# Output projection as seven half-size products over pairs of token blocks, in a hybrid decoder layer

## The chip, the cores and the metric

The kernel runs on one core of a Trainium2 chip (trn2). The metric is the device time of one execution in microseconds (us). Engines: TensorE (PE, its weight loads PEld), VectorE (DVE), ScalarE (ACT), GpSimd (POOL) and SyncE (SP), which here only issues DMAs. Each engine works through its own queue in order.

## What is computed

One layer of a decoder with two token mixers side by side, T = D = 1024, all in float32:

```
h = rmsnorm(x, norm_g);  proj = h @ w_in          # q, k, v, gates, decay code, merge gates
y_a = (gla(...) * silu gate) @ w_pa               # gated linear attention, 4 heads
y_b = (stick_breaking(...) * silu gate) @ w_pb    # 8 heads
merged = g_a * y_a + g_b * y_b
out = rmsnorm(x + merged @ w_o, final_g)
```

The change concerns `merged @ w_o` and what follows, and where its operands are made.

## The kernel before

Every float32 operand of a large product is split into a high part (ScalarE copies it as fp32r, `split` line 153) and a low part (VectorE subtracts, line 154); a product is then three matmuls, high x high, high x low and low x high. Activations are kept as four quarters of 512 x 512: two halves of the tokens by even and odd blocks of 128 rows of D (`quarter`, `quads_in`).

The stages in order of time: norm and value projections (to about 210 us); the **pair stage**, in which 24 `pair_job`s compute 256 columns of `proj` each (to about 730 us); the stick-breaking stage (`scores`, `turn`, `values`), with the w_pa product beside it; the **w_pb stage** (`m_half`, line 989, 16 units of 24 matmuls), and the **w_o stage** (from line 1002).

A `pair_job` (line 218) already computes its product by seven half-size products instead of eight, with sums of weights and sums of activations (T1 to T4, S1 to S4): `load` loads 1 MB of w_in into `raw` and makes four sums on GpSimd into `tt` (lines 228 to 231; there is one `tt` buffer, so the sums wait until VectorE has split those of the job before), and `unit(0..6)` are seven products of twelve matmuls. `Pairs.run` (line 65) hands out units, splits and loads. `pairs.run(24)` (line 619) runs the first 24 units; then the gated linear attention (GLA) begins between further units: `gl_half` (line 647) loads `qe` and `ke` and lets GpSimd multiply `qe` into `q2` (line 658), `gl_local` (line 673) begins with the products `pa` (lines 678, 679), of which every first one needs `q2` and `ke`.

Where no `manual_schedule` stands, a scheduler places the instructions of an engine, by its own estimate of when they are ready; with it an engine keeps the order of the program. A pool that is closed gives its memory to the next one; a new tile waits only for the users of the tiles that lay in the same place (`reuse_waits="tile"`).

In the w_o stage of before, the 128 tokens of a block are the stationary operand and w_o moves past: first 256 columns for all eight blocks (`proj_n`, lines 205 to 207), then 512 and 256 columns for each. `finish` (line 1019) adds x, squares for the norm, multiplies by final_g; then come the power on GpSimd (line 1043), the scaling and the stores.

Of the kernel before, what the change touches and what calls it, by code (L numbers as in the profile page):

```python
# [15 lines left out]
P = 128  # L16
# [78 lines left out]
def hybrid_layer(ctx: ExitStack, tc: tile.TileContext, x, norm_g, w_in, w_up, b_dec,  # L95
# [20 lines left out]
    def dram_set(nm, count, shape, dt=F32):  # L116
        return [dram.tile(shape, dt, tag=f"{nm}{i}", name=f"d_{nm}{i}") for i in range(count)]
# [10 lines left out]
    d_a21 = dram_set("a21", 2, [P, 4, HALF])  # L128

# [489 lines left out]
    pairs.run(24)  # L619
# [337 lines left out]
    pq = ctx.enter_context(tc.tile_pool(name="pq", bufs=1, reuse_waits="tile"))  # L957
    pb_ctx = ExitStack()
# [5 lines left out]
    mq = {}  # L964
# [22 lines left out]
    mq.update(quads_in(a21b, "m"))  # L987

    def m_half(pt, eb, n):
        o = stage().bitcast(F32)  # L990
# [20 lines left out]
    wB = [[po.tile([P, D - DV], F32R, tag=f"wo{s}{k}", name=f"wo{s}{k}", bufs=1) for k in range(KB)]
          for s in "hl"]
    ygA = po.tile([P, NT, DV], F32, tag="ygA", name="ygA", bufs=1)
    for kb in range(KB):
        raw = raw_tile().rearrange("p a b -> p (a b)")[:, 0:D - DV]
        nc.sync.dma_start(raw, w_o[kb * P:(kb + 1) * P, DV:D])
        split(raw, wB[0][kb], wB[1][kb])

    def finish(tb, k, c0, pt, y, yg):

        n = y.shape[-1]
        nc.vector.tensor_add(y, pt, y)
        junk = ps.tile([P, HALF], F32, tag="tr", name="junk")
        nc.scalar.activation(junk[:, 0:n], y, AF.Square, accum_out=ssq[:, tb, k:k + 1])
        nc.vector.tensor_mul(yg, y, fg[:, c0:c0 + n])

    for tb in range(NT):
        finish(tb, 0, 0, proj_n(wsA, mq, tb), xA[:, tb], ygA[:, tb])
    for tb in range(NT):
        ts = slice(tb * P, (tb + 1) * P)  # L1030
        y = po.tile([P, D - DV], F32, tag="y", name="y")
        nc.sync.dma_start(y, x2[ts, DV:D])
        yg = po.tile([P, D], F32, tag="yg", name="yg")
        nc.gpsimd.tensor_copy(yg[:, 0:DV], ygA[:, tb])
        for k, (c0, n) in ((1, (DV, HALF)), (2, (DV + HALF, DV))):
            a = c0 - DV
            pt = proj_n(lambda kb: (wB[0][kb][:, a:a + n], wB[1][kb][:, a:a + n]), mq, tb, n)
            finish(tb, k, c0, pt, y[:, a:a + n], yg[:, c0:c0 + n])
# [33 lines left out]
```

## Time and profile before

| | us |
|---|---|
| median of 3 timed runs (1262.37 to 1264.12) | 1262.98 |
| the profiled execution, its own time | 1259.98 |
| its span, first to last instruction | 1258.3 |
| TensorE busy | 1234.0 |
| VectorE busy | 753.4 |
| ScalarE busy | 519.8 |
| GpSimd busy | 243.3 |

Times of rows are microseconds from the start of the span. Matmuls overlap in a row's duration (0.39 us for 512 columns), so their pace is read from one start to the next. "[13.91 <-DVE wl L154]" behind a row is the idle time of its engine in front of it and what ended it. A granted clock of 1.00 is TensorE's full 2.4 GHz, 0.50 is its lower level, 1.2 GHz.

### The profile page before, as it was taken

How to read it: one execution, taken by the hardware profiler on the slowest of the kernel's cores; microseconds unless marked ns; L12 is line 12 of the kernel's file. 1: busy time of each engine (PE TensorE's matmuls, PEld its weight loads, DVE VectorE, ACT ScalarE, POOL GpSimd, SP SyncE). 2: the span in 40 equal slices, each digit the busy share in tenths (PEclk: the TensorE clock that was granted, in tenths of full speed). 3: DMA queues.
4: the chain of work that ended last, by engine and by line, in shares of the span. 5: the costliest groups of instructions: out<-in, count | busy, mean ns of one | idle time of the engine just before them, and what ended most of it. 6: DMA issues, size and time to landing. Idle time of an engine off the chain costs nothing.

```text
span 1258.3 us, 18805 instructions
## 1 busy us (share of the span) xinstructions
PE 1234.0 (98%) x6947; PEld 1054.5 (84%) x6947; DVE 753.4 (60%) x1309; ACT 519.8 (41%) x1024; POOL 243.3 (19%) x280
## 2 busy tenths in 40 slices
PE   8999999999999999999999999999999999999998
PEld 8999999888888888888888877777777878888986
DVE  5682454545667666666564357778887775444533
ACT  5454332344344444444444444545644443122322
POOL 2400471323223233232323010000100000000010
PEclk9999999999999999999999999999999999999999
DMA  7547353534644565655433765444775437543232
GB/s 270 186 142 269 126 181 133 188 116 149 192 157 137 188 208 173 215 179 177 159 117 121 246 206 160 135 163 147 220 245 175 135 109 265 190 161 110 85 116 92
DMA packets 176982, 212.09 MB, mean 169 GB/s; under 512 B 11222, under 2 KB 129004, under 8 KB 174332
## 3 DMA queue, kind: packets, MB, share of 16 engines
q1 hardware_dynamic: 175740, 209.34, 50.8%
q10 hardware_dynamic: 1152, 1.57, 0.3%
q8 instruction: 54, 0.88, 0.3%
q14 instruction: 36, 0.29, 0.1%
HBM read 133.28 MB, written 77.59 MB: 168 GB/s over the span
## 4 chain that ended last, share of the span: by engine, by line
PE 84%; DVE 8%; DMA 3%; ACT 2%; issue 2%; SPq 0%; POOL 0%; DVEq 0%; POOLq 0%; ACTq 0%
PE pp L254 12%; PE pp L256 12%; PE pp L255 12%; PE pp L207 7%; PE pp L205 7%; PE pp L206 7%; PE pp L193 6%; PE pp L194 6%; PE pp L192 5%; DVE eb L828 3%; PE av L864 1%; DVE be L833 1%; PE tr L847 1%; PE av L865 1%; PE av L863 1%
## 5 line engine op out<-in xcount | busy, mean ns | idle before, releaser
L153 ACT ACTIVATE wh<-raw 128x1024 fp32r<-128x1024 f32 x57 | 60.4, 1060 | 125.8 <-PE pp L193 69.6
L154 DVE TENSOR_TENSOR wl<-tt,wh 128x1024 fp32r<-128x1024 f32 x48 | 58.8, 1224 | 69.3 <-ACT wh L153 69.1
L291 DVE TENSOR_TENSOR f<-pp,f 128x512 f32<-128x512 f32 x72 | 49.7, 690 | 81.2 <-PE pp L256 77.9
L154 DVE TENSOR_TENSOR wl<-raw,wh 128x1024 fp32r<-128x1024 f32 x57 | 78.2, 1371 | 29.4 <-ACT wh L153 28.4
L153 ACT ACTIVATE wh<-tt 128x1024 fp32r<-128x1024 f32 x48 | 50.9, 1061 | 75.7 <-PE pp L255 69.0
L830 POOL TENSOR_SCALAR_AFFINE_SELECT be<-be 128x128 f32<-128x128 f32 x64 | 23.0, 360 | 277.1 <-ACT be L822 211.1
L828 DVE TENSOR_TENSOR_SCAN eb<-eb 128x128 f32<-128x128 f32 (+6 forms) x56 | 71.8, 1282 | 5.6 <-ACT eb L821 3.1
L154 DVE TENSOR_TENSOR o<-pp,o 128x256 fp32r<-128x256 f32 (+1 forms) x72 | 32.4, 451 | 66.1 <-ACT o L153 63.0
L153 ACT ACTIVATE o<-pp 128x256 fp32r<-128x256 f32 (+1 forms) x72 | 29.0, 403 | 93.5 <-PE pp L207 90.3
L821 ACT ACTIVATE eb<-z 128x384 f32<-128x384 f32 (+4 forms) x96 | 48.4, 506 | 44.6 <-PE z L819 30.7
L260 ACT ACTIVATE f<-pp 128x512 f32<-128x512 f32 x72 | 42.5, 590 | 55.8 <-PE pp L256 55.8
L228 POOL TENSOR_TENSOR tt<-raw 128x512 f32<-128x512 f32 x24 | 31.2, 1302 | 150.4 <-DVE wl L154 135.8
L153 ACT ACTIVATE ath<-tr 128x512 fp32r<-128x512 f32 (+2 forms) x96 | 44.0, 496 | 38.8 <-PE tr L847 37.9
L215 POOL TENSOR_TENSOR r<-r,nhalf 128x1 f32<-128x1 f32 x40 | 23.4, 586 | 188.3 <-DVE r L214 188.3
L154 DVE TENSOR_TENSOR atl<-tr,ath 128x512 fp32r<-128x512 f32 (+2 forms) x96 | 51.1, 546 | 5.3 <-ACT ath L153 5.3
L864 PE MATMUL av<-atl,v 128*128 128x256 f32 x160 | 47.0, 293 | 3.9 <-DVE atl L154 3.9
L847 PE MATMUL tr<-ident,be 128*128 128x128 f32 x288 | 44.5, 278 | 5.8 <-DVE be L833 4.9
L847 PEld LDWEIGHTS tr<-ident,be 128*128 128x128 f32 x288 | 32.5, 140 | 20.7 <-DVE be L833 11.2
L192 PE MATMUL pp<-bh,wh 128*128 128x512 f32 x128 | 49.9, 390 | 0.0
L193 PE MATMUL pp<-bl,wh 128*128 128x512 f32 x128 | 49.9, 390 | 0.0
L194 PE MATMUL pp<-bh,wl 128*128 128x512 f32 x128 | 49.9, 390 | 0.0
L833 DVE TENSOR_TENSOR be<-be,eb 128x128 f32<-128x128 f32 (+3 forms) x64 | 48.3, 755 | 1.9
(406 smaller groups left out, 4177.2 us busy)
## 6 DMA issues: line engine op xcount, KB each, us to landing
raw<-in_w_in_dram SPq DMA_DIRECT2D x31, 1024.0 KB, 5.9
d_v<-o SPq DMA_DIRECT2D x32, 256.0 KB, 3.2
d_gv<-o SPq DMA_DIRECT2D x16, 512.0 KB, 2.7
v<-d_gv SPq DMA_DIRECT2D x32, 256.0 KB, 3.1
d_q<-o SPq DMA_DIRECT2D x16, 512.0 KB, 5.7
d_k<-o SPq DMA_DIRECT2D x16, 512.0 KB, 3.9
k<-d_k SPq DMA_DIRECT2D x8, 1024.0 KB, 5.0
v<-d_v SPq DMA_DIRECT2D x8, 1024.0 KB, 6.6
```

The costliest lines, as they stand in the source:

```text
L153: nc.scalar.activation(hi, src, AF.Copy)
L154: eng.tensor_sub(lo, src, hi.bitcast(F32))
L192: nc.tensor.matmul(pt, whi[:, kb], h_, start=kb == 0, stop=False)
L193: nc.tensor.matmul(pt, whi[:, kb], l_, start=False, stop=False)
L194: nc.tensor.matmul(pt, wlo[:, kb], h_, start=False, stop=kb == KB - 1)
L205: nc.tensor.matmul(pt[:, 0:n], h_, whi, start=kb == 0, stop=False)
L206: nc.tensor.matmul(pt[:, 0:n], h_, wlo, start=False, stop=False)
L254: nc.tensor.matmul(pt, bh[:, j], ah[:, j], start=first and j == 0, stop=False, skip_group_check=True)
L255: nc.tensor.matmul(pt, bh[:, j], al[:, j], start=False, stop=False, skip_group_check=True)
L256: nc.tensor.matmul(pt, bl[:, j], ah[:, j], start=False, stop=j == 3, skip_group_check=True)
L828: nc.vector.tensor_tensor_scan(rest, rest, rest, om[:, T - P:T - P + 1], op0=ALU.mult, op1=ALU.min)
L847: nc.tensor.transpose(pt[:, b * P:(b + 1) * P], be[:, c:c + P], ident)
```

## The change

The product `merged @ w_o` is now made as in a pair job, for all tokens: with the four quarters of `merged` (A11, A12, A22 and the sums S1 to S4) as stationary and those of w_o (B11, B21, B22 and the sums T1 to T4) as moving operands, seven products of 512 x 512 x 512, each in four items of twelve 512-column matmuls (one item for each block of 128 tokens of a half). The fourth product (S1 T1) and the fifth (S4 B22) alternate.

The sums T1 to T4 of w_o are made in the first 24 units of the pair stage: w_o comes in four pieces of 1 MB (pairs of row blocks) into the new pool `tq`, GpSimd makes four subtractions in each and the results go to DRAM. GpSimd keeps program order there. Sums S1 to S4 of `merged` are made on GpSimd in the w_pb stage, whose last units change places, and go through DRAM too. In the last stage loads, splits and evictions are placed by hand between the items.

```diff
-    pairs.run(24)
...
+    tq_ctx = ExitStack()
+    tq = tq_ctx.enter_context(tc.tile_pool(name="tq", bufs=2, reuse_waits="tile"))
...
+    def t_sums(j, part):
+        a = wt[j]
+        for dst, x1, x2_ in (((0, 1, 0), (1, 3, 1)), ((3, 3, 0), (2, 2, 3)))[part]:
+            nc.gpsimd.tensor_sub(a[:, dst], a[:, x1], a[:, x2_])
+
+    def t_store(j):
+        for i, nm in enumerate(("T1", "T3", "T4", "T2")):
+            nc.sync.dma_start(d_t[nm][j // 2][:, j % 2], wt[j][:, i])
...
+        for at, fn in ((0, lambda j: t_load(j)), (5, lambda j: t_sums(j, 0)), (6, lambda j: t_sums(j, 1)),
+                       (8, lambda j: t_store(j))):
+            tjobs[5 * j + at].append((fn, j))
+    with tc.manual_schedule(engines={mybir.EngineType.Pool}):
+        for jobs in tjobs:
+            pairs.run(1)
+            for fn, j in jobs:
+                fn(j)
+    tq_ctx.close()
...
+        m = ms[j, n, e] = mo.tile([P, HALF], F32, tag="m", name="m")
         nc.vector.tensor_mul(o[:, 0], pt, o[:, 0])
-        nc.vector.tensor_add(o[:, 0], o[:, 0], o[:, 1])
-        q = mq[n, eb % 2]
-        split(o[:, 0], q[0][:, eb // 2], q[1][:, eb // 2])
+        nc.vector.tensor_add(m, o[:, 0], o[:, 1])
+        if n == 0:
+            hi, lo = op[("A11", "A12")[e]]
+            split(m, hi[:, j], lo[:, j])
...
+    def m_sums(j):
+        return [m_sum(j, "S1", (1, 0), (1, 1), ALU.add), m_sum(j, "S2", "S1", (0, 0), ALU.subtract),
+                m_sum(j, "S4", (0, 1), "S2", ALU.subtract), m_sum(j, "S3", (0, 0), (1, 0), ALU.subtract)]
...
+    def y_load(n, t):
+        ys[n, t] = (po.tile([P, D], F32, tag="ya", name="ya", bufs=4) if n == 0 or t == 3 else
+                    py.tile([P, D], F32, tag="y", name="y"))
+        r0 = n * HALF + t * P
+        nc.sync.dma_start(ys[n, t], x2[r0:r0 + P, :])
...
+    def product(bank, a, b, t, first):
+        (ah, al), w = op[a], op[b]
+        cs = slice(t * P, (t + 1) * P)
+        for j in range(4):
+            bh, bl = (v[:, j % 2] for v in w[j // 2]) if isinstance(w, list) else (v[:, j] for v in w)
+            nc.tensor.matmul(bank, ah[:, j, cs], bh, start=first and j == 0, stop=False, skip_group_check=True)
+            nc.tensor.matmul(bank, ah[:, j, cs], bl, start=False, stop=False, skip_group_check=True)
+            nc.tensor.matmul(bank, al[:, j, cs], bh, start=False, stop=j == 3, skip_group_check=True)
...
+    items = ([(u, t) for u in range(3) for t in range(4)] + [(3, 0), (3, 1), (4, 0), (3, 2), (4, 1), (3, 3), (4, 2), (4, 3)] +
+             [(u, t) for u in (5, 6) for t in range(4)])
...
+    for k, it in enumerate(items):
+        item(*it)
+        mine = [items[e] for e in ev_at.get(k, [k])]
+        for e in mine:
+            evict_a(*e)
+        for e in late:
+            evict_c(*e)
+        for nm, js in parts.get(k, []):
+            o_lo(nm, js)
+        if k in loads:
+            o_load(*loads[k])[0]()
+        his(k + 1)
+        for e in mine:
+            evict_b(*e)
+        late = mine
+        if k == 15:
+            y_load(1, 3)
```

`evict_a` adds an item's bank to the rows of x (VectorE) and squares finished halves (ScalarE), `evict_b` makes the factor of the norm, `evict_c` scales by it and by final_g and stores. `parts` and `loads` say after which item an operand is split and loaded.

How the instructions move. GpSimd at the second pair job of before (`tt` are a job's four sums, `q` is q2, `tri` and `am` are masks of the GLA):

```order
L625 MEMSET tri 128x128
L630 MEMSET am_3022 64x64
L630 MEMSET am_3023 64x64
L626 AFFINE_SELECT tri<-tri 128x128
L228 TENSOR_TENSOR tt<-raw 128x512
L230 TENSOR_TENSOR tt<-raw 128x512
L229 TENSOR_TENSOR tt<-raw,tt 128x512
L231 TENSOR_TENSOR tt<-raw,tt 128x512
L658 TENSOR_TENSOR q_3033<-qe,fac 128x512
```

and the same engine now, from the fifth pair job's sums on (`t` are the sums of w_o):

```order
L231 TENSOR_TENSOR tt<-raw 128x512
L232 TENSOR_TENSOR tt<-raw,tt 128x512
L233 TENSOR_TENSOR tt<-raw 128x512
L234 TENSOR_TENSOR tt<-raw,tt 128x512
L637 TENSOR_TENSOR t<-t 128x512 x8
L659 MEMSET tri 128x128
L664 MEMSET am_3091 64x64
L664 MEMSET am_3092 64x64
L660 AFFINE_SELECT tri<-tri 128x128
L692 TENSOR_TENSOR q_3102<-qe,fac 128x512
L231 TENSOR_TENSOR tt<-raw 128x512
```

The masks and q2 stood right behind the sums of the second pair job; they now stand behind those of the fifth and eight subtractions for w_o.

SyncE at the loads of `qe` and `ke` before (`f`, `d_e`: decay factors; `d_gq`, `d_gk`: q and k of the GLA in DRAM):

```order
L583 DMA f_2724<-d_e20_128 128x512
L656 DMA qe_3260<-d_gq0_116 128x512
L585 DMA d_gk0_120<-f_2724 128x512
L657 DMA ke_3034<-d_gk0_120 128x512
L583 DMA f_2778<-d_e21_129 128x512
```

(`qe` there is the second half's; the first one's load is twelve rows up) and now, with what each waits for:

```order
L607 DMA d_ga0_144<-o_3057 128x512 [waits DMAHW0_49,Activation_49]
L641 DMA d_tT11_171<-t_2914 128x512 [waits DMAHW1_49,Pool_49]
L641 DMA d_tT31_175<-t_2914 128x512 [waits DMAHW2_49,Pool_49]
L641 DMA d_tT41_177<-t_2914 128x512 [waits DMAHW3_49,Pool_49]
L641 DMA d_tT21_173<-t_2914 128x512 [waits DMAHW4_49]
L690 DMA qe_3101<-d_gq0_116 128x512 [waits DMAHW7_49,DMAHW6_49,DMAHW5_49]
L691 DMA ke_3103<-d_gk0_120 128x512 [waits DMAHW3_49,DMAHW4_49,DMAHW2_49,DMAHW1_49]
L700 DMA v_3107<-d_gv0_132 128x512
```

Both loads went behind the stores of the w_o sums (`d_tT`), and `ke` waits for four of them (the semaphores DMAHW1 to DMAHW4).

TensorE at the GLA's first product before (`S3`, `S4`, `ha22`: the fifth to seventh unit of the fourth pair job):

```order
L254 MATMUL pp_2959<-S3h_1595,wh_2955 128x512
L255 MATMUL pp_2959<-S3l_1596,wh_2955 128x512
L256 MATMUL pp_2959<-S3h_1595,wl_2956 128x512
L678 MATMUL pa_3081<-q2_3033,ke_3034 64x128
L679 MATMUL pa_3081<-qe_3032,ke_3034 64x64
L691 MATMUL tr_3092<-ident_170,k2_3090 128x128
L254 MATMUL pp_3042<-S4h_1703,dh_2935 128x512
L255 MATMUL pp_3042<-S4l_1704,dh_2935 128x512
```

and now:

```order
L258 MATMUL pp_3111<-S4l_1722,dh_2994 128x512
L259 MATMUL pp_3111<-S4h_1721,dl_2995 128x512
L257 MATMUL pp_3020<-ha22h_220,wh_3016 128x512
L258 MATMUL pp_3020<-ha22l_221,wh_3016 128x512
L712 MATMUL pa_3150<-q2_3102,ke_3103 64x128
L713 MATMUL pa_3150<-qe_3101,ke_3103 64x64
L259 MATMUL pp_3020<-ha22h_220,wl_3017 128x512
L257 MATMUL pp_3020<-ha22h_220,wh_3016 128x512
L725 MATMUL tr_3161<-ident_188,k2_3159 128x128
```

`pa` stood between the fifth and the sixth unit; it now stands behind the second matmul of the seventh.

SyncE at the end of the kernel before (`y`: rows of x):

```order
L1046 DMA out_dram<-yg 128x640
L1032 DMA y<-in_x_dram 128x768
L1046 DMA out_dram<-yg 128x640
L1032 DMA y<-in_x_dram 128x768
L1046 DMA out_dram<-yg 128x640
L1032 DMA y<-in_x_dram 128x768
L1046 DMA out_dram<-yg 128x640 x3
```

and now (`ya`, `y`: rows of x, in which the output is made):

```order
L1079 DMA raw<-d_sA_186 128x1024
L1079 DMA raw<-d_sA_187 128x1024
L1183 DMA out_dram<-ya 128x1024
L1137 DMA ya<-in_x_dram 128x1024
L1183 DMA out_dram<-ya 128x1024 x3
L1183 DMA out_dram<-y 128x512 x3
L1183 DMA out_dram<-ya 128x512
```

One load of x stands between the first and the second store of the output; the others come before all stores.

## Rows read from the trace of the kernel before

**Rows 1.** The page: busy time, share of the span and instructions of each engine; and the chain of work that ended last, by engine.

```profile
PE 1234.0 (98%) x6947; PEld 1054.5 (84%) x6947; DVE 753.4 (60%) x1309; ACT 519.8 (41%) x1024; POOL 243.3 (19%) x280
...
PE 84%; DVE 8%; DMA 3%; ACT 2%; issue 2%; SPq 0%; POOL 0%; DVEq 0%; POOLq 0%; ACTq 0%
```

**Rows 2.** The table of busy times by stretch: most of the w_pb stage, and the later part of the w_o stage. Columns: stretch, its length, then for each engine the busy time and (x) its instructions; granted clock, DMA share, GB/s.

```profile
1062.00:1158.00 96.00, 96.00 (x425) 79.51 (x424) 42.28 (x56) 18.80 (x24) 0.00 (x0) 1.00 0.50 165
1180.00:1252.00 72.00, 72.00 (x423) 63.42 (x421) 27.14 (x58) 15.12 (x43) 6.23 (x13) 1.00 0.24 84
```

**Rows 3.** The timeline of TensorE: the last 30 matmuls of the w_pb stage from their first, the first of the w_o stage, the first of a group of 24 matmuls of 512 columns in it and the first of the 256-column group behind, and the last matmul of the kernel. Columns: start, duration, engine, line, operation, out<-in, shape.

```profile
1154.62 0.39 PE L192 MATMUL pp<-bh,wh 128*128 128x512 f32 x1
...
1161.19 0.39 PE L194 MATMUL pp<-bh,wl 128*128 128x512 f32 x1
1161.42 0.28 PE L205 MATMUL pp<-wh,ma11h 128*128 128x256 f32 x1
...
1235.10 0.39 PE L205 MATMUL pp<-woh,ma21h 128*128 128x512 f32 x1
...
1240.67 0.28 PE L205 MATMUL pp<-woh,ma21h 128*128 128x256 f32 x1
...
1251.85 0.28 PE L207 MATMUL pp<-woh,ma22l 128*128 128x256 f32 x1
```

**Rows 4.** The timeline of the other engines at the end: a 512-column piece (add, square, the next small operation), and the last piece up to its scaling.

```profile
1249.31 0.69 DVE L1022 TENSOR_TENSOR y<-pp,y 128x512 f32<-128x512 f32 x1 [3.10 <-PE pp L207]
...
1250.04 0.60 ACT L1024 ACTIVATE junk<-y 128x512 f32<-128x512 f32 x1 [3.77 <-DVE y L1022]
...
1250.80 0.21 DVE L1040 TENSOR_SCALAR pre<-ssq 128x1 f32<-128x1 f32 x1
...
1252.16 0.42 DVE L1022 TENSOR_TENSOR y<-pp,y 128x256 f32<-128x256 f32 x1 [1.15 <-PE pp L207]
...
1253.16 0.21 DVE L1042 TENSOR_SCALAR r<-ssq,pre 128x1 f32<-128x1 f32 x1
1253.52 0.55 POOL L1043 TENSOR_TENSOR r<-r,nhalf 128x1 f32<-128x1 f32 x1 [7.90 <-DVE r L1042]
...
1254.10 0.61 ACT L1047 ACTIVATE yg<-yg,r 128x384 f32<-128x384 f32 x1 [0.97 <-POOL r L1043]
```

**Rows 5.** The timeline of TensorE: the first matmul of the pair stage, the first product of the GLA, and the first matmul of the seventh unit of the fourth pair job.

```profile
209.65 0.40 PE L254 MATMUL pp<-ha11h,wh 128*128 128x512 f32 x1
...
280.49 0.32 PE L678 MATMUL pa<-q,ke 128*64 128x128 f32 x1
...
283.75 0.39 PE L254 MATMUL pp<-ha22h,wh 128*128 128x512 f32 x1
```

**Rows 6.** The timeline of GpSimd: one sum of the first pair job, and the first and the last of the four sums of the fifth.

```profile
165.31 1.75 POOL L230 TENSOR_TENSOR tt<-raw 128x512 f32<-128x512 f32 x1
...
269.25 1.30 POOL L228 TENSOR_TENSOR tt<-raw 128x512 f32<-128x512 f32 x1 [13.91 <-DVE wl L154]
...
273.12 1.29 POOL L231 TENSOR_TENSOR tt<-raw,tt 128x512 f32<-128x512 f32 x1
```

**Rows 7.** The timelines of SyncE, GpSimd and VectorE around the GLA's first loads: a store to DRAM and the load that waits for it, for qe and for ke, and the first user of each.

```profile
216.83 0.32 SPq L585 DMA_DIRECT2D d_gq<-f  x1
218.84 0.32 SPq L656 DMA_DIRECT2D qe<-d_gq  x1
...
222.02 1.79 POOL L658 TENSOR_TENSOR q<-qe,fac 128x512 f32<-128x512 f32 x1 [5.96 <-DMA qe<-d_gq]
...
236.87 0.32 SPq L585 DMA_DIRECT2D d_gk<-f  x1
238.87 0.32 SPq L657 DMA_DIRECT2D ke<-d_gk  x1
...
241.88 0.28 DVE L688 TENSOR_TENSOR k<-ke,fac 128x128 f32<-128x128 f32 x1
```

**Rows 8.** The DMA issues by line (count, KB each, median us from issue to landing), and for ke's loads the shortest, median and longest.

```profile
xt<-in_x_dram SPq DMA_DIRECT2D x8, 512.0 KB, 7.5
...
y<-in_x_dram SPq DMA_DIRECT2D x8, 384.0 KB, 3.0
out_dram<-yg SPq DMA_DIRECT2D x8, 320.0 KB, 3.0
...
DMA to landing us min/median/max: 2.6/3.6/7.5
```

**Rows 9.** The table by stretch (columns as in rows 2; the granted clock is the third number from the end) after the last matmul, and the timeline of TensorE's first matmuls in the kernel, which only keep it busy (`warm`).

```profile
1254.00:1255.00 1.00, 0.00 (x0) 0.00 (x0) 0.55 (x1) 0.61 (x1) 0.07 (x1) 1.00 0.00 0
1255.00:1256.00 1.00, 0.00 (x0) 0.00 (x0) 0.00 (x0) 0.00 (x0) 0.00 (x0) 0.62 0.49 189
1256.00:1257.00 1.00, 0.00 (x0) 0.00 (x0) 0.00 (x0) 0.00 (x0) 0.00 (x0) 0.50 0.91 335
...
1.43 5.31 PE L137 MATMUL warm<-ident 128*128 128x128 f32 x26 [1.43 <-POOL ident masks.py:199]
...
8.95 2.40 PE L137 MATMUL warm<-ident 128*128 128x128 f32 x20
```

**Rows 10.** VectorE: two splits of 1024 columns in the timeline, the first beside GpSimd's sums of rows 6; and the scaling of 1024 columns by a factor and a row, in the table of groups by line (busy time, mean ns of one).

```profile
273.30 2.20 DVE L154 TENSOR_TENSOR wl<-raw,wh 128x1024 fp32r<-128x1024 f32 x1
278.80 1.23 DVE L154 TENSOR_TENSOR wl<-tt,wh 128x1024 fp32r<-128x1024 f32 x1 [3.30 <-ACT wh L153]
...
L374 DVE SCALAR_TENSOR_TENSOR xs<-xt,r,gb 128x1024 f32<-128x1024 f32 x8 | 10.2, 1278 | 1.4 <-POOL r L215 1.4
```

More of the change, by code (lines that the diff above doesn't have):

```diff
@@ L962, in b_dma @@
         reload_dma((d_osb[2 * j], d_osb[2 * j + 1]), j)
-    mq = {}
     def pb_load(eb):
@@ L1013, in hybrid_layer @@
[L1013 to L1025, printed above, removed]
@@ new lines, in m_stores, with go, o_load @@
+    def m_stores(j, nms=("S2", "S1", "S4", "S3", "A22")):
+        def go():
+            for nm in nms:
+                nc.sync.dma_start(d_s[nm][j // 2][:, j % 2], ms[j, nm] if nm[0] == "S" else ms[j, 1, 1])
+        return (go, False)
+    WQ = {"B11": (0, 0), "B21": (1, 0), "B22": (1, 1)}
+    def o_load(nm, tag="raw", js=(0, 4)):
+        def go():
+            raw = (raw_tile().rearrange("p k c -> p (k c)") if tag == "raw" else
+                   sw.tile([P, 4, 4, P], F32, tag="tt", name="tt", bufs=1).rearrange("p q a c -> p (q a c)"))
+            oraw[nm] = raw = raw.rearrange("p (j c) -> p j c", j=4)
+            for i in range(2):
+                n = min(js[1] - 2 * i, 2)
+                if nm in WQ:
+                    e, J = WQ[nm]
+                    src = (w_o.rearrange("(j two p) c -> two p j c", two=2, p=P)
+                           [e][:, 2 * i:2 * i + 2, J * HALF:(J + 1) * HALF])
+                else:
+                    src = (d_t if nm[0] == "T" else d_s)[nm][i][:]
+                nc.sync.dma_start(raw[:, 2 * i:2 * i + n], src[:, 0:n])
+        return (go, False)
@@ new lines, in hybrid_layer @@
+    for k, (eb, n) in enumerate(order):
+        if n == 0 and eb + 2 < KB:
+            line.append(pb_load(eb + 2))
+        line.append(pb_unit(eb, n))
+        if k % 4 == 3:
+            line += m_sums(k // 4)
+        if k % 4 == 0 and k:
+            line.append(m_stores(k // 4 - 1))
+        line += extra.get(k, [])
+    Line(line).run()
+    pb_ctx.close()
+    mo_ctx.close()
+    po = ctx.enter_context(tc.tile_pool(name="po", bufs=1, side="right", reuse_waits="tile"))
+    py = ctx.enter_context(tc.tile_pool(name="py", bufs=3, reuse_waits="tile"))
@@ new lines, in fresh_bank, with add, square, factor @@
+    def fresh_bank():
+        return ps.tile([P, HALF], F32, tag="pp", name="pp", bufs=3)
+    def add(n, t, J, bank):
+        y = ys[n, t][:, half(J)]
+        nc.vector.tensor_add(y, bank, y)
+    def square(n, t, J):
+        i = n * 4 + t
+        junk = ps.tile([P, HALF], F32, tag="av", name="junk", bufs=1)
+        nc.scalar.activation(junk, ys[n, t][:, half(J)], AF.Square, accum_out=ssq[:, i, J:J + 1])
+    def factor(n, t, J):
+        i = n * 4 + t
+        if (n, t) not in pre:
+            pre[n, t] = pq.tile([P, 2], F32, tag="pre", name="pre", bufs=8)
+            nc.vector.tensor_scalar(pre[n, t][:, 0:1], ssq[:, i, J:J + 1], D * EPS, None, op0=ALU.add)
+        else:
+            r = pre[n, t][:, 1:2]
+            nc.vector.tensor_scalar(r, ssq[:, i, J:J + 1], pre[n, t][:, 0:1], 1.0 / D, op0=ALU.add, op1=ALU.mult)
+            nc.gpsimd.tensor_tensor(r, r, nhalf, op=ALU.pow)
@@ new lines, in put, with scale, evict_a @@
+    def put(n, t, eng, cols):
+        r0 = n * HALF + t * P
+        eng.dma_start(o2[r0:r0 + P, cols], ys[n, t][:, cols])
+    def scale(n, t, cols):
+        y = ys[n, t][:, cols]
+        nc.vector.scalar_tensor_tensor(y, y, pre[n, t][:, 1:2], fg[:, cols], op0=ALU.mult, op1=ALU.mult)
+    WHERE = [(0, 0), (0, 0), (0, 1), (1, 1), (0, 1), (1, 1), (1, 0)]
+    def evict_a(u, t):
+        n, J = WHERE[u]
+        add(n, t, J, zb.pop(t) if u in (1, 4) else zb[t] if u == 3 else xb[t])
+        if u in (1, 4, 5, 6):
+            square(n, t, J)
@@ new lines, in item, with t3 @@
+    def item(u, t):
+        if u in (1, 3):
+            zb[t] = fresh_bank()
+        bank = zb[t] if u in (1, 3, 4) else xb[t]
+        product(bank, *(("A11", "B11"), ("A12", "B21"), ("S2", "T2"), ("S1", "T1"), ("S4", "B22"), ("S3", "T3"),
+                        ("A22", "T4"))[u], t, u in (0, 1, 3))
+    def t3():
+        return [tuple(sw.tile([P, KB, P], F32R, tag=tag, name=tag).rearrange("p k c -> p (k c)")
+                      .rearrange("p (j c) -> p j c", j=2) for tag in ("wh", "wl")) for _ in range(2)]
@@ L1051 @@
+    manual.close()
 _INS = ["x", "norm_g", "w_in", "w_dec_up", "b_dec", "gla_norm_g", "w_pa", "w_pb", "b_gate",
```

131 lines of the change are left out of this document (97 added, 34 removed).

## Prediction

> **What bounds the kernel now.** First the page's busy times and its chain of waits: TensorE is busy 98% of the span and the chain that ended last runs over it for 84% [rows 1]. Then the table by stretch: in the w_pb stage and in the w_o stage TensorE is busy all the time at full granted clock, while VectorE fills less than half of either [rows 2]. So what counts is how many matmuls there are, how far apart they start, and each stall of TensorE's queue, which works in program order. Nothing behind a stalled matmul can overtake it.
>
> **What the change removes.** In the timeline of TensorE the w_o stage begins at 1161.42 and its last matmul starts at 1251.85, which with its own 0.12 is 90.55 us [rows 3]. It has 8 token blocks x 8 row blocks x 3 = 192 matmuls of 512 columns and 384 of 256. The new stage has 7 products x 4 token blocks x 4 x 3 = 336 matmuls of 512 columns and nothing else. What one costs: in the stage just before, which is a pure stream of 512-column matmuls, 30 of them take 1161.42 - 1154.62 = 6.80 us, 0.2267 each; in the mixed stream of the old w_o stage 24 took 1240.67 - 1235.10 = 5.57, 0.2321 each [rows 3]. The new stream is pure, so I take 0.2267: 76.2 us. The other end is 78.0. Term: **-14.4**, up to -12.6.
>
> **The tail.** Before, the add started 0.31 after the start of the last matmul; the final scaling starts at 1254.10, 2.13 after the end of the matmuls at 1251.97, and takes 0.61: 2.74 [rows 4]. Now the last piece has 512 columns: 0.2, add 0.69, square until the next small VectorE operation 0.76 (1250.04 to 1250.80), from there to the power on GpSimd 0.36 and to the scaling 0.58, scaling 0.69 [rows 4]: 3.3. Term: **+0.6**. Output DMAs are of the same size as before.
>
> **Sums of w_o in the pair stage.** Sixteen GpSimd subtractions, 4 MB loaded and 4 MB stored. GpSimd waited 13.91 us in front of one of the pair jobs' sums [rows 6], so their time would be free. Their place is not. As the order shows, GpSimd now does the eight subtractions of the third and fourth pair of w_o rows right behind the sums of the fifth pair job, and the first multiplication of the gated linear attention (GLA) behind them; SyncE issues the GLA's loads of qe and ke behind the stores of these sums, ke even waits until the last store has landed, since it takes the same memory. Before, qe was loaded at 218.84 and ke at 238.87 [rows 7].
> By rows: the fifth job's sums start at 269.25, set off by VectorE freeing their buffer, which the change does not move, and end at 273.12 + 1.29 = 274.41, 5.16 for four [rows 6]. Eight more end at 284.7. Two stores are then issued, the second at 285.2. A store of that size lets a load that waits for it go 2.0 us later (216.83 to 218.84, 236.87 to 238.87), and ke's first user ran 3.0 us after its issue [rows 7]: ke is there at 290.2. qe is issued at 285.6, its multiplication starts 3.2 later (218.84 to 222.02 [rows 7]) and takes 1.3 as the sums do: ready at 290.1, no later than ke.
> TensorE arrives earlier. The pair stage starts at 209.65 [rows 5]; a unit of twelve matmuls is 2.72 us. The GLA's first product now stands behind two matmuls of unit 28, 27 x 12 + 2 = 326 matmuls after the start: 283.55. (Before it stood at 280.49, with its operands long there [rows 5].) It waits 290.2 - 283.55 = 6.7 us, with all matmuls behind it. With the shortest landing of ke, 2.6 [rows 8], it is 6.3; with ke's median of 3.6 for both the store and the load, 8.9. No later wait of TensorE is there to give this back. Term: **+6.7**.
> One row speaks for more: a split took 2.20 beside a GpSimd sum and 1.23 alone [rows 6, 10]. The Trainium skill ("SBUF — State Buffer", section "Who interferes with whom") says that a VectorE operation with two inputs in SBUF and a GpSimd operation that reads SBUF exclude each other for a whole instruction; the row agrees. By the sums' usual 1.29 the change stays at the sum below, by that rule it is the second rival.
> After the last matmul of the kernel, which starts at 1251.85, the granted clock is full until 1255, 0.62 in the next microsecond and then 0.50: the lower level, 1.2 GHz [rows 3, 9]. A stall of 6.7 us is twice as long as that, so I expect it to drop here too. What it costs to come back: at the start of the kernel 26 records of small matmuls took 5.31 us, later 20 took 2.40 [rows 9]; at the later pace 26 take 3.12, so 2.2 were lost. Term: **+2.2**, from 0 to 2.7 (half of the 5.31).
>
> **The new last stage.** Work beside the matmuls: VectorE 28 adds of 0.69 [rows 4], about 18 splits of 1.23 and 4 of 0.69, 4 scalings of 1.28 [rows 10], 8 passes of 0.69 and small ones, some 58 us of 76: hidden, and most splits are due three or more units (8 us) after their turn. One wait is added that can't be hidden. The row block (token block 3 of the second half) of x is loaded into the buffer of the first output block, so behind its store. With S the stage's start: unit 16 ends at S+43.5; VectorE adds (0.2 + 0.69), then scales the first output block (1.28 [rows 10]): S+45.7. Store, 3.0 to land, load, 3.0 [rows 8]: S+51.7; then VectorE's add of 0.69, which stands in front of the accumulation of unit 20, due at S+19 x 2.72 = S+51.7. Term: **+0.7**; at the top of the range 7.5 to land each way [rows 8], see below.
>
> **Taken as nothing.** In the w_pb stage GpSimd is idle and VectorE is busy 42.28 of 96 [rows 2]; sixteen sums on the one, and on the other four splits of 1.23 in place of eight of 0.69, are covered by the unit of 24 x 0.2267 = 5.4 us, and the first two sums of the last pair (2.6 us) are split only three items (8 us) into the new stage. If that cover were gone, TensorE would wait 1.23 for a late split. SyncE also loads the decay factors of the second pair job behind the stores of the first sums, so that VectorE multiplies later; the banks that it then frees late are taken again one to two units (3 to 5 us) on, which covers it, and uncovered it would cost about 2. At the start of the stick-breaking stage SyncE gets a 1 MB load of sums in front of the reloaded A21; TensorE there could wait about 1 us more or, with its changed order, 0.9 less. I take 0.
>
> **Sum.** -14.4 + 0.6 + 6.7 + 2.2 + 0.7 = -4.2. The profiled execution took 1259.98 us (span 1258.3 and 1.7 around it), so it becomes 1255.8. It is 3 us below the median of the timed runs, 1262.98, and I apply the difference there: **1258.8**. With the ends of the terms it runs from -7.5 (stall 6.3, no drop of the clock, transfer hidden) to +0.3 (0.2321, stall 8.9, clock 2.7): 1255.5 to 1263.3.
>
> **Rivals.**
> *The GLA's operands are in time.* Then -14.4 + 0.6 + 0.7 = -13.1: 1249.9. For it: the order of TensorE's queue was laid out with the first product only two matmuls into that unit, as if ke were there. Against: twelve sums at 1.29 from 269.25 on leave no way. Chance 0.12.
> *VectorE and GpSimd hinder each other.* A split beside a GpSimd sum took 2.20 against 1.23 alone, and single sums 1.75 instead of 1.29 [rows 6, 10]. If all eight sums that hold up ke take 1.75, ke comes 3.7 us later: -4.2 + 3.7 = -0.5, 1262.5, no change. Against: VectorE had only two splits between 273 and 281, and GpSimd's sum beside the first kept its 1.29 [rows 6, 10]. Chance 0.18.
> *The buffer of the first output block comes late.* Store and load of 512 KB each, one behind the other, at the 7.5 us that such loads took at the kernel's start [rows 8], would hold up unit 20 by 0.7 + 9.0 = 9.7, and -4.2 + 9.0 = +4.8: 1267.8, slower. From 6.7 us more than I count it is slower than the bound below. For it: both stand in one queue with other stores; against: the medians of 3.0 late in the kernel. Chance 0.1.
>
> **How the numbers follow.** The forecast has 0.6. About 0.2% (2.5 us) is what a measurement of this kernel can tell from no change. Faster by more: the first rival's 0.12, some two thirds of the forecast's (0.41) and a little of the second rival's: 0.56. Slower by more: the third rival's 0.1 and 0.06 from the upper ends of the others: 0.16. The rest is 0.28. The range of 1253 to 1265 leaves out most of the first rival (0.1) and of the third (0.08).
>
> **What would show it.** Right: one idle of TensorE of 6 to 9 us near 284, released by the DMA of ke or by the GpSimd multiplication, with granted clock 0.5 behind it; 336 matmuls at 0.227 in about 76 us; one wait of about a microsecond some 50 us into that stage, released by VectorE behind the load of x. Wrong: no idle near 284 (then it is near 1250), a pace of 0.232, splits that TensorE waits for in the last stage, or new waits in the stick-breaking stage.

## The result, and the profile after

The changed kernel takes 1267.29 us (median of 11 runs, 1264.51 to 1269.59), the kernel before in the same comparison 1262.99 (1261.79 to 1264.12): ratio 1.0034, interval 1.0024 to 1.0044. It is slower by 0.34%; 1258.8 was predicted, in a range of 1253 to 1265. The profiled execution took 1264.65 us.

The page after, to be held against [rows 1], and the table of waits of TensorE (what waited, for what; us in total, times, longest):

```profile
PE 1224.5 (97%) x6707; PEld 1037.8 (82%) x6707; DVE 774.5 (61%) x1301; ACT 525.9 (42%) x1012; POOL 293.9 (23%) x304
...
PE 81%; DVE 8%; DMA 4%; issue 3%; ACT 2%; POOL 2%; SPq 0%; DVEq 0%; ACTq 0%; POOLq 0%
...
PE pa L712 <- DMA ke<-d_gk: 5.7, 1, 5.7
PE pp L257 <- DVE f L294: 5.6, 2, 3.0
...
PE pp L1153 <- DVE ya L1162: 0.8, 1, 0.8
```

TensorE has 240 matmuls and 9.5 us of work less, and the span is 4.6 longer. The chain of waits now runs over DMA and GpSimd for 6%, before for 3%. All three lines of waits are new. The next table gives the stages, between starts of matmuls in the timelines. The pair stage runs from its first matmul to the first product of scores, the stick-breaking stage from there to the last product of values. Then come 119.8 us in each of these kernels, and the last stage, from its first matmul to its last. The further profiles of both kernels are from below:

| | pair | stick-breaking | last | profiled execution |
|---|---|---|---|---|
| before | 522.4 | 309.5 | 90.4 | 1259.98 |
| before, again | 522.5 | 312.3 | 90.4 | 1262.89 |
| before, third | 522.9 | 312.9 | 90.4 | 1263.97 |
| after | 536.5 | 312.6 | 77.0 | 1264.65 |
| after, again | 536.6 | 314.1 | 77.2 | 1266.44 |

The mean granted clock of the changed kernel's executions runs from 0.993 in the shortest to 0.989 in the longest. The last stage gives what it was meant to give, and the pair stage takes it back. TensorE there, against [rows 5], then the stretch of the stall (clock third from the end):

```profile
253.27 0.50 PE L257 MATMUL pp<-ha12h,wh 128*128 128x512 f32 x1 [2.59 <-DVE f L294]
...
289.25 0.50 PE L257 MATMUL pp<-ha22h,wh 128*128 128x512 f32 x1 [3.04 <-DVE f L294]
289.59 0.39 PE L258 MATMUL pp<-ha22l,wh 128*128 128x512 f32 x1
295.65 0.44 PE L712 MATMUL pa<-q,ke 128*64 128x128 f32 x1 [5.67 <-DMA ke<-d_gk]
...
301.09 0.48 PE L257 MATMUL pp<-ha11h,wh 128*128 128x512 f32 x1
...
290.00:295.60 5.60, 0.00 (x0) 0.00 (x0) 0.76 (x5) 1.26 (x4) 1.57 (x4) 0.50 0.69 234
297.00:298.00 1.00, 1.00 (x5) 0.70 (x4) 0.60 (x2) 0.43 (x2) 0.00 (x0) 0.50 0.53 171
300.00:301.00 1.00, 1.00 (x7) 0.44 (x5) 0.00 (x0) 0.48 (x1) 0.00 (x0) 0.93 1.04 315
```

The `pa` that stood at 280.49 starts at 295.65, and behind it the clock stays at 0.50, 1.2 GHz, until about 300. Before it are two waits for VectorE. What the other engines did then, against [rows 6, 7], and behind it two rows of the kernel before:

```profile
238.07 0.32 SPq L641 DMA_DIRECT2D d_tT<-t  x1
...
244.33 0.38 SPq L588 DMA_DIRECT2D d_gk<-f  x1
245.98 0.81 SPq L631 DMA_DIRECT2D t<-in_w_o_dram  x2
246.83 1.42 SPq L586 DMA_DIRECT2D f<-d_e  x3
...
251.92 0.69 DVE L587 SCALAR_TENSOR_TENSOR f<-f 128x512 f32<-128x512 f32 x1 [8.59 <-DMA f<-d_e]
...
269.78 1.06 ACT L156 ACTIVATE wh<-tt 128x1024 fp32r<-128x1024 f32 x1 [0.39 <-PE pp L258]
270.87 1.23 DVE L157 TENSOR_TENSOR wl<-tt,wh 128x1024 fp32r<-128x1024 f32 x1 [0.44 <-ACT wh L156]
272.18 1.30 POOL L231 TENSOR_TENSOR tt<-raw 128x512 f32<-128x512 f32 x1 [2.89 <-DVE wl L157]
277.30 12.56 POOL L637 TENSOR_TENSOR t<-t 128x512 f32<-128x512 f32 x8
...
285.83 4.85 SPq L641 DMA_DIRECT2D d_tT<-t  x4
287.00 0.15 DVE L678 MEMSET fac<- 128x48 f32 x2 [3.60 <-DMA d_tT<-t]
290.78 0.40 SPq L690 DMA_DIRECT2D qe<-d_gq  x1
292.69 0.32 SPq L691 DMA_DIRECT2D ke<-d_gk  x1
```

```profile
239.24 1.38 SPq L583 DMA_DIRECT2D f<-d_e  x3
...
266.85 1.06 ACT L153 ACTIVATE wh<-tt 128x1024 fp32r<-128x1024 f32 x1 [1.22 <-PE pp L255]
```

Read from the top: SyncE issues the four stores of the first sums as GpSimd makes them, then waits with the load of the third piece until its buffer is free, and only then loads the decay factors, at 246.83 (before 239.24). VectorE stands 8.59 us in front of them, and TensorE loses 2.59 for a bank that VectorE frees behind them. From there on TensorE is 2.9 late, and it hands this on: ScalarE copies the fourth job's `tt` when a matmul lets it, at 269.78 (before 266.85), VectorE's split that frees `tt` follows at 270.87, and the sums of the fifth pair job start at 272.18 and not at 269.25. From there it is the chain of the prediction, 5.4 us later at its end. In it VectorE also stops at its memset of `fac` (a small tile of the GLA in the memory of the pieces of w_o) until a store has landed, and TensorE's wait of 3.04 is for a bank behind that.

The last stage and the end, against [rows 3, 4]:

```profile
1178.61 0.39 PE L1153 MATMUL xb<-wB11h,mA11h 128*128 128x512 f32 x1
...
1231.26 0.50 PE L1153 MATMUL pp<-wB22h,mS4h 128*128 128x512 f32 x1 [0.81 <-DVE ya L1162]
...
1255.65 0.39 PE L1155 MATMUL xb<-wT4h,mA22l 128*128 128x512 f32 x1
...
1258.55 0.72 ACT L1211 ACTIVATE ya<-ya,pre 128x512 f32<-128x512 f32 x1 [0.42 <-POOL pre L1179]
```

### The profile page after: what moved, and what is told of

The parts are those of the page before. It is cut to its first block, busy times and chain, and to the rows that moved or that the text cites. A ratio compares the mean times of both kernels' runs of the same rounds, so it can differ in the third digit from the quotient of the medians.

```text
span 1262.9 us, 18427 instructions
## 1 busy us (share of the span) xinstructions
PE 1224.5 (97%) x6707; PEld 1037.8 (82%) x6707; DVE 774.5 (61%) x1301; ACT 525.9 (42%) x1012; POOL 293.9 (23%) x304
## 4 chain that ended last, share of the span: by engine, by line
PE 81%; DVE 8%; DMA 4%; issue 3%; ACT 2%; POOL 2%; SPq 0%; DVEq 0%; ACTq 0%; POOLq 0%
PE pp L257 11%; PE pp L259 11%; PE pp L258 11%; PE pp L197 6%; PE pp L196 6%; PE pp L195 6%; PE pp L210 4%; PE pp L208 4%; PE pp L209 4%; DVE eb L862 3%; DMA q<-d_q 2%; PE av L898 1%; PE tr L881 1%; PE av L899 1%; PE xb L1154 1%
```

## The experiments

**Without the sums, and the sums alone.** The first kernel replaces the pieces, sums and stores of w_o by the `pairs.run(24)` of before and loads quarters of w_o as T1 to T4; the second is the kernel before with only these sums in its pair stage.

```diff
-    wt = {}
...
+    pairs.run(24)
...
-    WQ = {"B11": (0, 0), "B21": (1, 0), "B22": (1, 1)}
+    WQ = {"B11": (0, 0), "B21": (1, 0), "B22": (1, 1),
+          "T1": (0, 0), "T2": (0, 1), "T3": (1, 0), "T4": (1, 1)}
```

> The changed kernel without the sums of w_o in the pair stage: their loads, GpSimd subtractions and stores are left out, and the last stage loads quarters of w_o in place of T1 to T4, so the output is not the layer's. Theory (queue and memory): the three waits of TensorE in the pair stage (2.59, 3.04 and 5.67 us) and the half clock behind them (about 2.2) all come from these sums, so all 13.5 us go: 1267.3 - 13.5 = 1253.8, and the first product of the GLA stands where it stood before. Rival (the new last stage is slower than it looks, or something else of the change costs): less than 10 us come back. On the stick-breaking stage, which took 3.1 us more in the changed kernel: if that comes from the sums or from the shift they cause, it goes too, 1250.7; if it comes from the rest of the change, it stays.

> The kernel before with the sums of w_o in its pair stage and nothing else of the change; the sums are stored and never used. Theory (queue and memory): the pair stage loses what it loses in the changed kernel, 13.5 us, and the last stage is the old one: 1263.0 + 13.5 = 1276.5. Rival (the loss is not made by these sums alone): under 1270. If the 3.1 us of the stick-breaking stage come with the sums, 1279.6.

Measured: 1252.17 (ratio 0.9913, 0.9896 to 0.9929) and 1279.66 (1.0126, 1.0108 to 1.0145). The pair stages take 522.5 and 536.3, the stick-breaking stages 313.5 and 313.3. In the first, the sums of the fifth pair job are back at their time, and the unit that holds the stall takes 3.27 us instead of 11.84:

```profile
269.27 1.30 POOL L231 TENSOR_TENSOR tt<-raw 128x512 f32<-128x512 f32 x1 [13.90 <-DVE wl L157]
283.78 0.39 PE L257 MATMUL pp<-ha22h,wh 128*128 128x512 f32 x1
...
287.05 0.48 PE L257 MATMUL pp<-ha11h,wh 128*128 128x512 f32 x1
```

So these sums make the whole loss of the pair stage, and the rest of the change is worth 10 us.

**Is it the traffic, or what stands behind it?** Four kernels, each built on an earlier one, take one more thing away. The first has a pool of its own for the GLA's first operands:

```diff
+    gw = gl_ctx.enter_context(tc.tile_pool(name="gw", bufs=2, reuse_waits="tile"))
...
-        qe, q2, ke = (gv.tile([P, HALF], F32, tag=t, name=t) for t in ("qe", "q2", "ke"))
+        qe, q2, ke = (gw.tile([P, HALF], F32, tag=t, name=t) for t in ("qe", "q2", "ke"))
```

> The changed kernel with one difference: qe, ke, q2, the masks and the factors of the GLA lie in a pool of their own (gw), outside the memory that the pieces of w_o had. Theory (queue and memory): the scheduler is then free to place the loads of qe and ke ahead of the stores, TensorE's first product of the GLA goes back to its old place, and the waits of 3.04 and 5.67 us and the half clock behind them (2.2) go; the wait of 2.59 for the decay factors stays: 1267.3 - 10.9 = 1256.4. Rival (traffic: 8 MB more of DMA and the GpSimd sums beside VectorE slow everything there): the waits only move, over 1262.

Measured: 1272.7 (1.0070, 1.0055 to 1.0085), slower than the change itself; the expectation failed. `pa` is early now (286.53), but right behind it stands the transposition of `k2`, and `k2` still lay in the pieces' memory:

```profile
296.24 0.29 DVE L723 TENSOR_TENSOR k<-ke,fac 128x128 f32<-128x128 f32 x1 [9.72 <-DMA d_tT<-t]
296.58 0.48 PE L726 MATMUL tr<-ident,k 128*128 128x128 f32 x1 [9.62 <-DVE k L723]
```

> As the kernel with a pool of its own for the operands of the GLA, and in addition the loads of the decay factors are issued by ScalarE's queue instead of SyncE's, so that they do not stand behind the stores of the sums. Theory (queue and memory): the wait of 2.59 us near 253 goes as well: 1267.3 - 13.5 = 1253.8. Rival (traffic): that wait stays, no faster than the kernel with its own pool alone.

Here `nc.scalar.dma_start(e, d_e[h]...)` stands in place of `nc.sync`, on top of the pool `gw`. Measured: 1266.9 (1.0035, 1.0019 to 1.0051), not the 1253.8 expected. The wait near 253 is gone, as expected; but the `k2` wait stays (5.04), and ScalarE stands 6.51 us in front of a staging tile whose store is behind the sums' stores in SyncE's queue:

```profile
274.40 0.60 ACT L594 ACTIVATE o<-pp 128x512 f32<-128x512 f32 x1 [6.51 <-DMA d_gg<-o]
...
275.54 0.80 PE L257 MATMUL pp<-S2h,wh 128*128 128x512 f32 x1 [3.16 <-ACT f L263]
```

The next kernel has `k2`, `as` and `kn` in `gw` too (and the decay factors loaded by SyncE again); the one behind it has `nc.gpsimd.dma_start(d_t[nm]...)` for the stores as well:

> As the kernel with a pool of its own for the GLA's operands, but now k2 and the splits of the masked product and of k (as, kn) lie outside the memory of the w_o pieces too; only tiles that are needed later (v, the gates, the state) lie in it. In the kernel with the first pool, TensorE waited 9.62 us for a transposition of k2, which VectorE could not write before the last store of the sums had landed. Theory (memory): that wait and the half clock behind it go, and only the wait of some 4 us for the decay factors near 254 stays: the kernel without the sums took 1252.2, so 1256.5. Rival (traffic, or yet another wait behind the stores in SyncE's queue): over 1260.

> The kernel before this one, with the stores of the sums of w_o issued by GpSimd's own queue, right behind the sums, so that nothing in SyncE's queue stands behind them but the loads of the next pieces. Theory (SyncE's queue): the decay factors come in time and no wait is left in the pair stage: 1252.2, as without the sums. Rival (GpSimd pays for the issues, or the loads of the next pieces hold up SyncE in the stores' place): 1256 or more.

Measured: 1267.12 (1.0031, 1.0017 to 1.0044) and 1260.34 (0.9977, 0.9964 to 0.9990); both miss what was expected, 1256.5 and 1252.2. In the first, ScalarE's split of q2 into `qs`, in the pieces' memory as well, waits 11.07 for the stores, and what VectorE makes behind it comes late: TensorE waits 4.91 at 299.16 and 4.20 for the decay factors. In the second the decay factors are in time, and what is left is the load of `v`, again in that memory:

```profile
302.78 0.55 PE L733 MATMUL pu<-v,knh 128*128 128x256 f32 x1 [3.64 <-DMA v<-d_gv]
```

**The same work at another time.** In the w_pb stage, in the free buffer `tt`, or in its old place with the GLA eight units later, the last also with the last two pieces loaded by GpSimd:

```diff
+        wt[j] = sw.tile([P, 4, 4, P], F32, tag="tt", name="tt", bufs=1).rearrange("p q a c -> p q (a c)")
...
+    pairs.run(8)
     tq_ctx.close()
...
+            (nc.sync if j < 2 else nc.gpsimd).dma_start(wt[j][:, 2 * two:2 * two + 2],
```

> The changed kernel with the sums of w_o in another place: in the buffer of the pair jobs' sums (tt), which is free after the pair stage, one piece after the other, made on GpSimd in program order between the units of the w_pb stage (some of the first piece may come at the start of the stick-breaking stage). Theory (the place is what costs, not the sums): the pair stage has no wait left and the w_pb stage keeps its 119.8 us from the last product of the stick-breaking stage to the first of the last stage: 1252.2. Rival (SyncE's queue is held up there as well, its loads for the merge come late and TensorE waits in the w_pb stage): 1256 or more, up to the 1267 of the changed kernel.

> The changed kernel with eight more units of the pair jobs ahead of the GLA (32 in place of 24); the sums of w_o, their memory and their queue stay as they are. By the profile of the changed kernel the last store of the sums has landed at about 292.7 and unit 32 begins at 209.7 + 32 x 2.72 = 296.7 and the 2.6 us of the wait for the decay factors, 299.3. Theory (the GLA's first tiles lie in the memory of the sums, so it may not begin before the last store has landed): the waits of 3.04 and 5.67 us and the half clock go, only the wait for the decay factors stays: the kernel without the sums took 1252.2, so 1254.8. Rival (traffic; or three units behind the GLA are too few to load the first head of the stick-breaking stage): 1259 or more.

> As the kernel with the later GLA, and the third and fourth piece of w_o are loaded by GpSimd's queue, so that the loads of the decay factors do not stand behind them in SyncE's queue; the stores stay there. In the changed kernel SyncE had the last of the four stores issued at 244.2 and waited until 246.0 with the load of the third piece, whose buffer was not free. Theory (SyncE's queue): the decay factors are loaded 2.1 us earlier and TensorE's wait near 253 shrinks from 2.6 to 0.5: about 1252.8. Rival (the wait is for the transfer, or the issues cost GpSimd too much): no faster than the kernel with the later GLA alone.

Measured: 1266.17 (1.0026, 1.0011 to 1.0040), 1264.24 (1.0013, 0.9998 to 1.0027), 1263.46 (1.0002, 0.9989 to 1.0014): in all three the time fell to the rival. In the w_pb stage the loads for the merge (`o`) stand behind four stores in SyncE's queue just so. It costs TensorE 3.24 us there and, since the rows of x come late, 5.41 in the last stage; the stick-breaking stage of that profile is 318.6 too, for a reason that stays open:

```profile
1146.34 6.42 SPq L1050 DMA_DIRECT2D d_tT<-tt  x4
1152.80 0.46 SPq L1005 DMA_DIRECT2D o<-d_gb  x1
...
1157.69 0.76 PE L195 MATMUL pp<-bh,wh 128*128 128x512 f32 x1 [3.24 <-DVE o L1008]
1200.50 0.80 PE L1146 MATMUL pp<-wB21h,mA12h 128*128 128x512 f32 x1 [5.41 <-DVE ya L1155]
```

What the last of them was made to show did come: SyncE issues the decay factors at 244.78, the wait near 253 is gone, and the sums of the fifth pair job are back at their time:

```profile
269.27 1.29 POOL L231 TENSOR_TENSOR tt<-raw 128x512 f32<-128x512 f32 x1 [2.82 <-DVE wl L157]
```

But the time is lost elsewhere. A later GLA removes the wait for `ke`; the scheduler, however, puts GLA instructions into the queues ahead of the GLA's own units: the memset of `fac` stops VectorE again (TensorE 1.80 at 289.70), and ScalarE's split of q2 costs TensorE 1.90 at 300.06, with GpSimd's loads 4.43 at 297.90. The stick-breaking stage, now closer behind the GLA, begins below full clock (0.57 and 0.50 from 746 to 750) and takes 315.9 and 318.7.

**Early sums.** The first kernel has GpSimd's order set by hand, the stores and the last two loads issued by GpSimd, and the GLA's tiles in `gw`; the second has the memory as in the changed kernel:

```diff
+    for at, todo in ((0, (t_load, 0)), (1, (t_load, 1)), (5, (t_sums, 0, 0)), (6, (t_sums, 0, 1)), (6, (t_store, 0)),
+                     (6, (t_sums, 1, 0)), (7, (t_sums, 1, 1)), (7, (t_store, 1)), (7, (t_load, 2)), (8, (t_load, 3)),
+                     (9, (t_sums, 2, 0)), (9, (t_sums, 2, 1)), (10, (t_store, 2)),
+                     (11, (t_sums, 3, 0)), (11, (t_sums, 3, 1)), (12, (t_store, 3))):
```

> All sums of w_o stay in the pair stage, with the same subtractions, loads and stores, but: GpSimd makes those of the second piece right behind those of the first and those of the third and fourth ahead of the sums of the fifth pair job; it issues the stores and the last two loads itself, right where they fall in its order; and the GLA's first tiles lie outside the pieces' memory (as in the kernel with k2, as and kn there). Theory (the loss is made by what waits in SyncE's queue and by the memory, and the traffic costs nothing): by the durations in the profile with GpSimd's stores (sums 1.29 each, a group of four issues 2.2) all sums and stores are done by about 272 and landed by 275, no wait is left in the pair stage, it takes 522.4 us, and the kernel takes what it takes without the sums, 1252.2, at most 1254. Rival (8 MB more of traffic, or GpSimd beside VectorE, has a price of its own): at least 1257, with waits of TensorE for splits or sums between 240 and 280.

> As the kernel before this one, but the memory stays as in the changed kernel: the GLA's tiles lie where the pieces of w_o lay. Theory: since the last store has landed by about 275, qe and ke can be loaded then and are there by 278 to 279, ahead of TensorE's first product of the GLA at 280.5; q2 has to wait on GpSimd for the sums of the fifth pair job or comes ahead of them. So the order and the queue alone do nearly all: 1252 to 1255. Rival (the memory is what counts): a wait of 5 us or more near 281, 1257 or more.

Measured: 1267.57 (1.0042, 1.0028 to 1.0055) and 1265.34 (1.0020, 1.0010 to 1.0030), both far off. The first has one wait of TensorE in the pair stage, and it is the memory once more: ScalarE stands still in front of the split into `qs`. The profile puts that down to GpSimd, but the tile lies in the memory of the pieces, whose last store was issued by 280.5, and with `qs` out of that memory the wait is gone (the kernel after the next).

```profile
284.67 0.51 ACT L156 ACTIVATE qsh<-q 128x128 fp32r<-128x128 f32 x2 [15.53 <-POOL tt L233]
285.72 0.79 PE L257 MATMUL pp<-S2h,wh 128*128 128x512 f32 x1 [12.90 <-ACT f L263]
```

In the second it is the memory and GpSimd's order. VectorE stops 7.59 us at the memset of `fac` for a store of the sums, and ScalarE 14.45 in front of a split of q2, which GpSimd multiplies only behind the fifth job's sums. TensorE waits 4.65 at 279.82 and 4.11 at 289.43.

```profile
276.65 0.16 DVE L679 MEMSET fac<- 128x48 f32 x2 [7.59 <-DMA d_tT<-t]
...
287.77 0.31 ACT L156 ACTIVATE qsh<-q 128x128 fp32r<-128x128 f32 x1 [14.45 <-POOL q L693]
```

Then `qs` went out of that memory, and last GpSimd's fourth piece came behind the fifth pair job's sums (with `v` and the gates in the memory of the third piece):

```diff
-        pool = gw if tag in ("as", "kn") else gv
+        pool = gw if tag in ("as", "kn", "qs") else gv
...
-                     (11, (t_sums, 3, 0)), (11, (t_sums, 3, 1)), (12, (t_store, 3))):
+                     (15, (t_sums, 3, 0)), (15, (t_sums, 3, 1)), (16, (t_store, 3))):
```

> The kernel with the early sums and GpSimd's stores, with one tile moved: the splits of q2 (qs) too lie outside the memory of the w_o pieces; to make room, qs and kn have one buffer each in place of two. In the run before, ScalarE, which keeps its order, stood from 269 to 284.7 in front of the first split into qs, until the last store of the sums had landed, and TensorE waited 12.9 us for a bank that ScalarE empties behind it. Theory (memory and queue only): that was the last such tile, the pair stage takes 522.4 us and at most 1 more, and the kernel 1252.2 to 1254. Rival (the traffic or the GpSimd sums have a price that no order removes, or the single buffers hold up the GLA): at least 1257.

> As the kernel before, but GpSimd makes the sums of the fourth piece behind those of the fifth pair job instead of ahead of them, and v and the gates of the GLA lie in the memory of the third piece, whose stores are done sooner. In the run before, GpSimd was busy 97% of the time from 250 to 280, so that the sums of the fifth pair job began at 281.6 instead of 269.3, and ScalarE waited 8.1 and TensorE 4.2 us for them. Theory (the sums cost nothing but what waits behind them, GpSimd's own time included): the sums of the fifth pair job begin at about 273.2, half a microsecond or so too late, no wait above 1 us is left, and the pair stage takes 524 us or less: 1252.5 to 1254.5. Rival (GpSimd beside the others or the traffic costs more than that): 1257 or more.

Measured: 1259.33 (0.9981, 0.9971 to 0.9991), then **1254.62** (0.9940, 0.9924 to 0.9956), against 1262.45 for the kernel before. The first misses its 1252.2 to 1254: GpSimd's own time was full. The second lies a little above its 1252.5 to 1254.5. GpSimd's first sum for the fifth pair job, who waited for it, and the stretch of GpSimd's work (its busy time the fifth), in the kernel with all early; and the same sum in the last kernel:

```profile
281.62 1.27 POOL L231 TENSOR_TENSOR tt<-raw 128x512 f32<-128x512 f32 x1
284.27 1.06 ACT L156 ACTIVATE wh<-tt 128x1024 fp32r<-128x1024 f32 x1 [8.07 <-POOL tt L232]
285.87 0.80 PE L257 MATMUL pp<-S4h,dh 128*128 128x512 f32 x1 [4.24 <-ACT f L263]
...
250.00:280.00 30.00, 29.85 (x132) 24.38 (x131) 19.00 (x16) 11.88 (x16) 29.25 (x28) 1.00 0.78 274
```

```profile
273.19 1.31 POOL L231 TENSOR_TENSOR tt<-raw 128x512 f32<-128x512 f32 x1
```

The last kernel's pair stage takes 524.95 us, 2.5 more than without the sums, with all of their subtractions, loads and stores in it. So the sums' work costs at most those 2.5; the other 11.5 us of the change's 14.0 went with the order, the queues and the memory. Even the 2.5 are mostly not from the time of the sums, whose last store is issued by 287.6: the 37th unit starts at 312.63, 102.94 us into the stage; without the sums it is 102.41, so 0.5 are lost by then. Of the other 2.0, 0.8 come between the 43rd and the 49th unit, where this wait stands:

```profile
339.67 0.33 PE L728 MATMUL tr<-ident,k 128*128 128x128 f32 x1 [0.44 <-DVE knl L157]
```

`kn` has one buffer in this kernel and two in the changed one; that this is the reason was not tested.

**How much differs from one execution to the next.**

> The kernel before, unchanged, profiled once more. The stick-breaking stage, from its first product of scores to its last product of values, took 309.5 us in the one profile of before, 312.6 in that of the changed kernel, 313.5 in that without the sums of w_o and 313.3 in that with these sums alone. Theory (it differs from one execution to the next, because a wait of about 2 us there lets the granted clock fall in some and not in others): this execution takes 311 or more, and shows a stretch below full clock. Rival (the change disturbs it): 309.5 again, within half a microsecond, at full clock.

> The changed kernel, unchanged, profiled once more. Theory (the pair stage loses the same in every execution, the stick-breaking stage varies): from the first product of the pair stage to the first of the scores 536.5 us again within 0.5, the last stage 77.0 again, and the stick-breaking stage anywhere from 309 to 315 us. Rival (the pair stage varies too, which would explain that its timed runs spread over 5 us): it differs by over 1 us.

> The kernel before, profiled a third time. Its stick-breaking stage took 309.5 and 312.3 us in the two profiles so far, that of kernels with a part of the change 311.8 to 314.7. Theory (chance from one execution to the next): between 309 and 315. Rival (the change adds a little of its own there): below 312.

Measured: the table at the top. The pair stage of the changed kernel is the same to 0.1 us. The stick-breaking stage of the kernel before is not: 309.5, 312.3 and 312.9, so the first profile caught a short one. The reason is not one and the same: the second profile has a clock of 0.66 from 932 to 937, while the third is at full clock in every 5 us of the stage and waits 4.2 us for loads (q and ha21) where the other two wait 1.3. In the changed kernel it took 312.6 and 314.1, and in the kernels that have the change or a part of it, with the GLA and the sums in the pair stage where they were, or without sums, 311.8 to 317.2. Whether the change adds a microsecond or two there stays open.

## Why the prediction was wrong, by its own steps

- *-14.4, the matmuls:* right. From its first matmul to the end of its last (0.23 behind 1255.65) the stage takes 77.27 instead of 90.55, with the wait of 0.81 in it; (77.04 - 0.81) / 335 = 0.2276 for one.
- *+0.6, the tail:* right, 1259.27 - 1255.88 = 3.4 instead of 3.3. (The output stores did not keep their size, 640 and 384 columns before, 512 and 512 now, but the time behind the last scaling is 3.6 in both.) *+0.7, the row block of x:* right, 0.81, released by VectorE where it was expected. The third rival's late buffer did not come.
- *+2.2, the clock:* right. The stalled unit takes 11.84 instead of 3.27; without the wait of 5.67 and a GLA group of 0.55 that stands elsewhere in the kernel without the sums, 2.35 is left.
- *+6.7, the stall:* wrong in size, right in place and cause. It ended at 295.65, not at 290.2. Of the 5.4 us, 2.9 are the sentence that the fifth job's sums start at 269.25, "set off by VectorE freeing their buffer, which the change does not move". The change does move it, since TensorE itself came late. 2.2 are the eight subtractions, 12.56 instead of 10.3, two of them at 2.27 and 2.15 while VectorE split. This is the second rival, at 2.2 of its 3.7. The Trainium skill says so ("SBUF — State Buffer", section "Who interferes with whom": one of the two waits for the other's whole instruction), and these rows agree. The idle of 6 to 9 us came as two, 3.04 and 5.67 with two matmuls between them.
- *Taken as nothing, the decay factors:* this is the step that failed first. The bank was not covered by "one to two units": it cost TensorE 2.59, and through TensorE's lateness, ScalarE's copy and VectorE's split the 2.9 above. Where the loads of these factors (or of the third and fourth piece) were taken out of SyncE's queue, or the stores, the wait near 253 was gone. I had followed SyncE's queue to ke, and not every other load behind the same stores, nor VectorE's queue behind the first of these loads. The memset of `fac` was missed too; it cost nothing of its own, since ke came later anyway.
- *The rest taken as nothing:* the w_pb stage keeps its 119.8; for the stick-breaking stage, whose start was put at 0, it stays open (above).
- *The step from the profile to the median:* the 3.0 us between them were the short stick-breaking stage of that one execution, so adding them was right.

With 14.1 for the pair stage in place of 8.9 the sum is +1.0 and not -4.2. The medians differ by 4.3. The other 3.3 were not found in one place: the profiled executions of the changed kernel were 1264.65 and 1266.44, below the middle of its timed runs, and no profile shows where the longest of them, at 1269.59 and a mean clock of 0.989, lose their time.

## What to carry to other kernels

Before work is put on an idle engine, list what its stores and loads stand in front of in the issuing queue, and what later takes the memory of its buffers; both lists must be followed through every in-order queue behind them, since the first operation that stops there holds up all others. One tile moved away only shows the next one: here ke, k2, v and qs in turn. In the last kernel the work itself cost little (0.5 us in its own time) once nothing waited behind it, and the same engine's time had then to be counted as well.

## What was not expected of the hardware

A kernel's own stages differ by 3.4 us between executions of the same program (309.5 to 312.9), nearly the 4.3 us by which the changed kernel is slower. A GpSimd-issued store occupied GpSimd for about 0.55 us (four in 2.17 to 2.35, in the kernel with GpSimd's stores), SyncE for 0.32 (median, in the changed kernel).
